# A Strassen level over half of the inner dimension in a gated linear recurrence, with gate functions moved between engines

## The chip, the cores and the metric

One core of a Trainium2 chip runs the whole program. The metric is the device time of one execution in microseconds. The kernel before took 2131.48 us (median of three runs, 2130.56 to 2131.69). Five engines with own instruction queues work in it: TensorE (PE in the profile, its weight loads PEld), VectorE (DVE), ScalarE (ACT), GpSimd (POOL) and SyncE (SP, which here issues DMAs).

## The reference

A decoder trunk of two layers on 1024 tokens of width 1024. The first layer mixes tokens with a gated linear recurrence (HGRN2), the second with sliding-window attention, and each ends with a gated convolutional FFN of width 2816. The change lies in the first mixer:

```python
q, f, i, g = jnp.split(h @ w_in, 4, axis=-1)          # h (1024, 1024), w_in (1024, 4096)
fg = lb + (1.0 - lb) * jax.nn.sigmoid(heads(f))       # 8 heads of 128
o = hgrn2_chunkwise(jax.nn.silu(heads(q)), 1.0 - fg, heads(i), jnp.log(fg))
o = o * lax.rsqrt(jnp.mean(jnp.square(o), -1, keepdims=True) + RMS_EPS)
o = o * g_norm_w * jax.nn.silu(heads(g))
return o.reshape(B, S, D) @ w_out
...
u = h @ w_in                                          # FFN: up, causal conv of width 3, gate, down
return (jax.nn.silu(a) * b) @ w_out
```

The recurrence is `S_t = diag(f_t) S_{t-1} + k_t v_t^T ; o_t = S_t^T q_t` with k = 1 - f and v = i.

## The kernel before

Everything is float32, and a product is made from float32r parts: a tile is split into a high part (ScalarE casts) and a low part (VectorE subtracts, `low_part`, L169), and `mm3` makes three passes hi x hi, hi x lo, lo x hi into one PSUM bank (L194, L195, L196). `T` holds x transposed, [128 of the inner dimension, part, 8 chunks, 1024 tokens], `HL` the split weights in six places, `raw` the three tiles into which weights are loaded. There are four PSUM banks of 512 columns (`psmm`) and two of 1024 (`psax`).

Stages: the start (x is transposed by TensorE in blocks of 128 tokens, `turn_block`, and each block cast and subtracted into T, while the i/g products of head 0 run), then the recurrence over eight heads, the out projection, the FFN of layer 0, attention, and the FFN of layer 1. In the recurrence TensorE makes for head h the projections `qf(h)` (queries and forget gates, transposed, two token halves each, 8 chunks x 3 passes per half), then `ig_block` (values and gates by token blocks, two passes per chunk, L714 and L715; the result is copied by ScalarE, added by VectorE, L677 and L679, and then its PSUM bank is free). Between these run the small matmuls of `recur(h - 1)` (L200): VectorE scales qp and kp from level to level of a binary tree over the 32-token blocks (`update`, L990 to L995), and TensorE makes `scores` of each level, whose results VectorE puts into Ab (L933, L954). At its end come the state sums (L1071, L1073), the output og, and `norm` (L1098 to L1109), for which GpSimd computes two small instructions.

Beside this the kernel prepares the weights of both FFN down projections for a Strassen product: 22 units of four 128 x 512 subtractions each, on VectorE (L1184), loaded into Y and stored to memory (`bsd`). They are spare work: `lay` puts one in where VectorE's planned backlog is short.

The order of all instructions is written out by hand by a planner (`Order`): `od.t` counts TensorE's time from column counts, `od.v` VectorE's backlog, generators are resumed when TensorE's time has come to the times that they yield, and the spare work fills VectorE while `od.v` is under `od.t + 1.5`. What it decides is fixed when the program is built; on the chip each engine runs its rows in this order and waits for semaphores.

## Time and profile before

| quantity | before |
|---|---|
| median of three runs | 2131.48 us |
| profiled execution | 2131.04 us, span 2129.3 us |
| granted TensorE clock | 1.00 |
| TensorE busy | 2119.9 us, 100% of the span |
| VectorE, ScalarE, GpSimd busy | 83%, 44%, 6% |
| stages by the rows | start to 37.6 us, heads to 456, out projection to about 500, then FFN, attention, FFN |
| one head | about 53 us |

A row of the timeline gives start, length, engine, line, operation, what is written from what, shape, and in brackets the idle time ahead of it with what ended it. A row of groups has the count behind x, then the busy time in all, the mean in ns and the idle time ahead. A row of waits has the sum, the count and the longest.

### The profile page before, as it was taken

The numbers are of one execution on the slowest core, as the hardware profiler recorded it, in microseconds if no ns is written. First come the engines' busy times: TensorE is split into PE (matmuls) and PEld (weight loads), VectorE is DVE, ScalarE is ACT, GpSimd is POOL, SyncE is SP. The second block draws the span as 40 slices with busy tenths as digits, with TensorE's granted clock in tenths as the row PEclk, the third lists the DMA queues.
The fourth block names the chain that finished last, engine by engine and source line by source line (L and its number), as shares of the span: only waits on it lengthen the run. The fifth ranks groups of instructions, "written<-read, shape, count | busy, mean of one in ns | idle before, by whom it ended". The sixth has DMA issues, their size and how long they took to land.

```text
span 2129.3 us, 32129 instructions
## 1 busy us (share of the span) xinstructions
PE 2119.9 (100%) x12663; PEld 1779.6 (84%) x12663; DVE 1760.9 (83%) x2375; ACT 926.5 (44%) x1491; POOL 132.5 (6%) x150
## 2 busy tenths in 40 slices
PE   9999999999999999999999999999999999999998
PEld 8888888888888888888888888888888888888887
DVE  4777776677999999887988658969999999978986
ACT  4444444452444444434433356743544444444430
POOL 1000000001100000000001113321000000000002
PEclk9999999999999999999999999999999999999999
DMA  5655443214223222228854411042233222249662
GB/s 216 243 211 169 144 132 119 75 32 177 99 85 98 85 89 79 80 99 275 288 190 161 129 26 45 24 149 89 80 100 98 90 86 83 86 148 325 229 215 90
DMA packets 229838, 278.96 MB, mean 131 GB/s; under 512 B 29960, under 2 KB 158648, under 8 KB 226872
## 3 DMA queue, kind: packets, MB, share of 16 engines
q1 hardware_dynamic: 228736, 276.53, 39.0%
q8 instruction: 99, 1.62, 0.3%
q10 hardware_dynamic: 856, 0.37, 0.1%
q14 instruction: 51, 0.42, 0.1%
q0 software_dynamic: 96, 0.02, 0.0%
HBM read 213.94 MB, written 62.94 MB: 130 GB/s over the span
## 4 chain that ended last, share of the span: by engine, by line
PE 99%; DMA 0%; DVE 0%; SPq 0%; issue 0%; DVEq 0%
PE psmm L194 17%; PE psmm L196 17%; PE psmm L195 17%; PE psax L194 10%; PE psax L196 10%; PE psax L195 10%; PE psmm L714 5%; PE psax L200 4%; PE psmm L715 3%; PE psmm L204 1%; PE psmm L200 1%; PE psax L204 1%; PE psax L1427 1%; PE psmm L1274 1%; DMA Y<-in_x_dram 0%; PE psmm L752 0%
## 5 line engine op out<-in xcount | busy, mean ns | idle before, releaser
L194 PE MATMUL psmm<-T,HL 128*128 128x512 f32 x768 | 303.4, 395 | 0.0
L196 PE MATMUL psmm<-T,HL 128*128 128x512 f32 x768 | 299.4, 390 | 0.0
L195 PE MATMUL psmm<-T,HL 128*128 128x512 f32 x768 | 299.2, 390 | 0.0
L473 DVE SCALAR_TENSOR_TENSOR Y<-Y,cwt 128x1023 f32<-128x1023 f32 (+1 forms) x176 | 225.0, 1281 | 44.3 <-ACT Y L471 42.9
L221 ACT CAST HL<-rx 128x1024 fp32r<-128x1024 f32 (+1 forms) x151 | 150.7, 1007 | 178.3 <-PE psmm L195 30.9
L169 DVE TENSOR_TENSOR HL<-rx,HL 128x1024 fp32r<-128x1024 f32 (+1 forms) x151 | 178.5, 1188 | 16.9 <-ACT HL L221 16.8
L714 PE MATMUL psmm<-HL,T 128*128 128x512 f32 x496 | 176.8, 399 | 0.0
L196 PEld LDWEIGHTS psmm<-T,HL 128*128 128x128 f32 x768 | 144.2, 188 | 30.7
L194 PEld LDWEIGHTS psmm<-T,HL 128*128 128x128 f32 x768 | 144.3, 188 | 29.6 <-issue 0.4
L195 PEld LDWEIGHTS psmm<-T,HL 128*128 128x128 f32 x768 | 144.3, 188 | 28.8 <-issue 0.4
L471 ACT ACTIVATE Y<-Y,cwt 128x1024 f32<-128x1024 f32 x88 | 108.7, 1238 | 101.6 <-DVE Y L460 89.4
L715 PE MATMUL psmm<-HL,T 128*128 128x256 f32 x496 | 138.9, 280 | 0.0
L194 PE MATMUL psax<-T,HL 128*128 128x512 f32 x352 | 137.3, 390 | 0.0
L196 PE MATMUL psax<-T,HL 128*128 128x512 f32 x352 | 137.0, 389 | 0.0
L195 PE MATMUL psax<-T,HL 128*128 128x512 f32 x352 | 137.0, 389 | 0.0
L243 POOL TENSOR_TENSOR rs<-rs,nhalf 128x1 f32<-128x1 f32 x32 | 44.6, 1394 | 1286.6 <-DVE rs L242 1286.6
L714 PEld LDWEIGHTS psmm<-HL,T 128*128 128x128 f32 x496 | 93.1, 188 | 21.0
L715 PEld LDWEIGHTS psmm<-HL,T 128*128 128x128 f32 x496 | 93.7, 189 | 0.4
L221 ACT CAST HT<-rx 128x1024 fp32r<-128x1024 f32 (+1 forms) x37 | 35.5, 960 | 127.9 <-DVE rx L427 76.4
L169 DVE TENSOR_TENSOR HL<-raw,HL 128x1024 fp32r<-128x1024 f32 x51 | 62.1, 1219 | 20.2 <-ACT HL L176 19.3
L195 PEld LDWEIGHTS psax<-T,HL 128*128 128x128 f32 x352 | 66.2, 188 | 13.7
L196 PEld LDWEIGHTS psax<-T,HL 128*128 128x128 f32 x352 | 66.1, 188 | 13.6
(315 smaller groups left out, 5232.3 us busy)
## 6 DMA issues: line engine op xcount, KB each, us to landing
rx<-in_ffn_w_in_dram SPq DMA_DIRECT2D x136, 256.0 KB, 3.2
rx<-gd SPq DMA_DIRECT2D x118, 256.0 KB, 3.9
Y<-in_ffn_w_out_dram SPq DMA_DIRECT2D x44, 512.0 KB, 6.4
bsd<-Y SPq DMA_DIRECT2D x22, 1024.0 KB, 4.8
gd<-Y SPq DMA_DIRECT2D x44, 512.0 KB, 2.6
rx<-in_ffn_w_out_dram SPq DMA_DIRECT2D x54, 256.0 KB, 4.7
R<-bsd SPq DMA_DIRECT2D x44, 256.0 KB, 5.1
Y<-in_ffn_w_in_dram SPq DMA_DIRECT2D x40, 256.0 KB, 2.9
```

Source lines behind the costliest of these rows:

```text
L169: make = lambda e: e.tensor_tensor(lo, src, hi.bitcast(F32), op=ALU.subtract)
L194: nc.tensor.matmul(ps, st(0), mv(0), start=start, stop=False)
L195: nc.tensor.matmul(ps, st(0), mv(1), start=False, stop=False)
L196: nc.tensor.matmul(ps, st(1), mv(0), start=False, stop=stop)
L200: nc.tensor.matmul(ps, lhsT, rhs, start=start, stop=stop, **kw)
L204: nc.tensor.transpose(ps, src, ident)
L221: nc.scalar.copy(hi, src)
L243: nc.gpsimd.tensor_tensor(rs, rs, nhalf, op=ALU.pow)
L471: nc.scalar.activation(c, u, AF.Identity, bias=cwt[:, l, 3, ci:ci + 1], scale=cwt[:, l, 2, ci:ci + 1])
L473: nc.vector.scalar_tensor_tensor(c[:, sh:], u[:, :S - sh], cwt[:, l, 2 - sh, ci:ci + 1], c[:, sh:], op0=ALU.mult, op1=ALU.add)
L714: nc.tensor.matmul(ps, T[:, 0, kc, ts], w[:, :, kc % 4, :], start=kc == 0, stop=False)
L715: nc.tensor.matmul(ps[:, :256], T[:, 1, kc, ts], w[:, 0, kc % 4, :], start=False, stop=kc == KC - 1)
```

## The change

Queries and forget gates of a head are made together. Over chunks 0 to 3 of the inner dimension, the product of x (two token halves by two pairs of chunks) with the weights (two pairs of chunks by q and f) is done by one Strassen level: seven products of two chunks instead of eight. Chunks 4 to 7 stay as they were. The PSUM tiles are pa, ps, pc, pd, and pa again: pa is begun, copied out, added on to, copied out, added on to, read by VectorE, and added on to once more for the late queries. The sums and differences of x are made once at the start, for blocks 4 to 7 while they are transposed: the chunks 0 and 1 of the late tokens hold in T the sum of two chunks, a new tile `Sx` holds three other sums, and GpSimd, VectorE and ScalarE share the work (`x_whole`, `x_sums`). So that i/g blocks can use this T, each head gets a weight difference (`ig_diff`); for the q/f weights there are four small VectorE sums (`qf_sums`), and each head splits one weight tile more of 512 and one of 768 columns.

Silu and Tanh on ScalarE take the place of Sigmoid and a VectorE product. The weight sums for the FFN work in half units in Yx, one row by VectorE as spare work (16 of 44 half units), the other by GpSimd (28), with loads and stores in quarters. Y's place is freed: the first six heads' outputs go to memory (`hod`) and come back into Sx in the last head, the seventh's stays in Yx, and the out projection takes the late token blocks first. The spare work fills up to 2.0 instead of 1.5.

```diff
-        while self.fill and self.v < self.t + 1.5 and self.fill():
+        while self.fill and self.v < self.t + 2.0 and self.fill():
...
+        def ig_diff(raw):
+            d = tail["raw"][2][:, :512]
+            nc.vector.tensor_tensor(d, raw[:, 512:], raw[:, :512], op=ALU.subtract)
+        def qf_sums(q, f):
+            b11, b21, b12, b22 = q[:, :256], q[:, 256:512], f[:, :256], f[:, 256:512]
+            t3, t2, t4 = [tail["raw"][2][:, 256 * i:256 * (i + 1)] for i in range(3)]
+            for x, y, z in ((t3, b22, b12), (b12, b12, b11), (t2, b22, b12), (t4, b21, t2)):
+                nc.vector.tensor_tensor(x, y, z, op=ALU.subtract)
...
                 yield 0.7
-                nc.scalar.activation(sg, G, AF.Sigmoid)
-                yield 0.8
-                nc.vector.tensor_tensor(G, G, sg, op=ALU.mult)
+                nc.scalar.activation(G, G, AF.Silu)
...
+            def x_whole(tb):
+                t0 = slice((tb - 4) * P, (tb - 3) * P)
+                raw = lambda h: T[:, h, :4, t0].bitcast(F32)
+                sub2(fours[tb % 2][0].rearrange("p (k t) -> p k t", k=KC)[:, :4], raw(0), raw(1), op=ALU.add)
+            def x_sums(tb):
...
+                nc.scalar.copy(r[:, 4:6], pv[:, :2])
+                split(T[:, 0, 2:, ts], T[:, 1, 2:, ts], pv[:, 2:])
+                nc.vector.tensor_tensor(r[:, 6:8], r[:, 4:6], pv[:, 2:4], op=ALU.add)
+                sub2(v[:, 1], r[:, :2], r[:, 4:6], op=ALU.subtract)
+                sub2(v[:, 0], r[:, 6:8], r[:, :2], op=ALU.subtract)
+                sub2(v[:, 2], r[:, 2:4], v[:, 0], op=ALU.subtract)
+                split(T[:, 0, :2, ts], T[:, 1, :2, ts], r[:, 6:8])
...
-            for half in range(2):
-                proj_T(weights["f"], half, ps)
-                nc.scalar.activation(fg[:, ts], ps, AF.Sigmoid)
...
+            pa = psmm()
+            add_on(pa, q, 0, tokens(early), 2, start=True)
+            nc.scalar.copy(kp[:, early], pa)
+            ps = psmm()
+            add_on(ps, q, 2, tokens(early, 2), 6, start=True)
+            after(1.0, query_early(ps))
+            add_on(pa, e, 2, sums(0), 2)
+            nc.scalar.copy(fg[:, early], pa)
+            pc = psmm()
+            add_on(pc, f, 0, tokens(late), 2, start=True)
+            nc.scalar.copy(fg[:, late], pc)
+            pd = psmm()
+            add_on(pd, f, 4, tokens(late, 4), 4, start=True)
+            add_on(pa, e, 0, sums(1), 2)
+            after(0.5, third(pa))
+            add_on(pc, f, 4, tokens(early, 4), 4, stop=False)
+            after(0.0, forget_late(pd))
+            add_on(pc, f, 2, sums(2), 2)
+            after(0.5, forget_early(pc))
+            od.finish(mine[1:2])
+            add_on(pa, e, 4, tokens(late, 2), 2, stop=False)
+            add_on(pa, q, 4, tokens(late, 4), 4)
+            nc.scalar.activation(qs[:, late], pa, AF.Silu)
...
+                for us, x, y, z in ((0.69, blocks[:, :2], blocks[:, 1::2], blocks[:, :2]), (0.42, b22, b22, b11), (0.42, b21, b21, b22)):
+                    if r:
+                        sub2(x, y, z, op=ALU.subtract)
+                    else:
+                        pending.append((us, lambda x=x, y=y, z=z: tt(x, y, z, op=sub)))
```

`sub2` is GpSimd's tensor_tensor, `plus` and `third` are VectorE adds of 512 columns (L1010), and `add_on` makes the three passes per chunk (L999).

The order of ScalarE at the start of before, from the cast of block 3 (psax_248) on; psax_292, psax_309 and psax_354 are blocks 4, 5 and 6:

```order
L221 CAST T_81<-psax_248 128x8x128
L696 ACTIVATE VG_169<-psmm_170 128x2x128
L697 COPY VG_169<-psmm_170 128x2x128
L221 CAST T_81<-psax_292 128x8x128
L677 COPY VG_169<-psmm_274 128x256
L221 CAST T_81<-psax_309 128x8x128
L677 COPY VG_169<-psmm_306 128x256
L687 ACTIVATE sg_344<-VG_169 128x256
L221 CAST T_81<-psax_354 128x8x128
```

The same place in the change, where psax_260, psax_308 and psax_334 are blocks 3, 4 and 5, and qs and VG_104 hold copies and sums of chunks:

```order
L221 CAST T_81<-psax_260 128x8x128
L176 CAST HL_82<-raw2_101 128x512
L726 ACTIVATE VG_180<-psmm_181 128x2x128
L727 COPY VG_180<-psmm_181 128x2x128
L836 COPY qs_128<-psax_308 128x256
L221 CAST T_81<-psax_308 128x6x128
L221 CAST T_81<-qs_128 128x2x128
L710 COPY VG_180<-psmm_289 128x256
L836 COPY VG_104<-psax_334 128x256
L221 CAST T_81<-psax_334 128x6x128
L221 CAST T_81<-VG_104 128x2x128
L221 CAST Sx_102<-fg_129 128x3x2x128
```

A block's one cast has become a copy and two casts with a VectorE sum between them; the weight difference's cast stands ahead of block 4, and the cast of the sums that GpSimd makes behind block 5.

The order of TensorE in the change where the second head's projection (psmm_1249 is pa, psmm_1306 pc) runs between two steps of the first head's scores (L200):

```order
L999 MATMUL psmm_1249<-Sx_102,HL_82 128x512 x3
L200 MATMUL psax_1342<-St_1188,one_112 32x256 x4
L200 MATMUL psax_1342<-VG_180,one_112 32x128 x4
L200 MATMUL psax_1342<-kd_1195,one_112 32x256 x4
L200 MATMUL psax_1342<-VG_180 32x16 x32
L200 MATMUL psax_1342<-qp_1184,kp_653 32x16 x32
L999 MATMUL psmm_1249<-Sx_102,HL_82 128x512 x3
L999 MATMUL psmm_1306<-T_81,HL_82 128x512 x12
L999 MATMUL psmm_1306<-Sx_102,HL_82 128x512 x6
L999 MATMUL psmm_1249<-T_81,HL_82 128x512 x3
L200 MATMUL psax_1471<-kd_1422 32x16 x32
```

Where before a projection went on through the passes of one bank, TensorE comes back to pa after 12 and 6 passes elsewhere. The order of VectorE in the change at this place, released by the small matmuls above (psax_1342):

```order
L1143 TENSOR_TENSOR qp_1184<-qp_1184,tot_1185 128x64x8
L1145 TENSOR_TENSOR kp_653<-kp_653,tot_1185 128x64x8
L1148 TENSOR_TENSOR tot_1185<-tot_1185 128x64
L1086 COPY_PREDICATED Ab_116<-msk_79,psax_1342 128x256
L1086 COPY_PREDICATED Ab_116<-msk_79,psax_1342 128x128
L1107 COPY_PREDICATED Ab_116<-msk_79,psax_1342 128x32x4
L1143 TENSOR_TENSOR qp_1184<-qp_1184,tot_1185 128x32x16
L1145 TENSOR_TENSOR kp_653<-kp_653,tot_1185 128x32x16
L1148 TENSOR_TENSOR tot_1185<-tot_1185 128x32
L1107 COPY_PREDICATED Ab_116<-msk_79,psax_1342 128x16x8
L1086 COPY_PREDICATED Ab_116<-msk_79,psax_1342 128x64x2 x2
L1010 TENSOR_TENSOR fg_1247<-fg_1247,psmm_1249 128x512
```

and of before, from its last update of the same kind on:

```order
L990 TENSOR_TENSOR qp_603<-qp_603,tot_604 128x32x16
L992 TENSOR_TENSOR kp_459<-kp_459,tot_604 128x32x16
L995 TENSOR_TENSOR tot_604<-tot_604 128x32
L954 COPY_PREDICATED Ab_113<-msk_79,psax_707 128x16x8
L933 COPY_PREDICATED Ab_113<-msk_79,psax_707 128x64x2 x2
L1184 TENSOR_TENSOR Y_82<-Y_82 128x512
L169 TENSOR_TENSOR HL_83<-raw1_100,HL_83 128x1024
```

Behind the same updates and copies, where a weight sum stood that nobody waits for, there is now the add that reads pa.

GpSimd's order, which in before had in the heads only the norm's pairs:

```order
L169 TENSOR_TENSOR HL<-raw_99,HL 128x1024
L1099 TENSOR_SCALAR ss<-ss 128x8
L1100 TENSOR_TENSOR ss<-ss,nhalf 128x8
L1099 TENSOR_SCALAR ss<-ss 128x8
L1100 TENSOR_TENSOR ss<-ss,nhalf 128x8
```

and in the change, from the second weight half unit that it sums to the norm of the first head:

```order
L1341 TENSOR_TENSOR Yx<-Yx 128x512
L1341 TENSOR_TENSOR Yx<-Yx 128x256 x2
L1341 TENSOR_TENSOR Yx<-Yx 128x512
L1341 TENSOR_TENSOR Yx<-Yx 128x256 x2
L1252 TENSOR_SCALAR ss<-ss 128x8
L1253 TENSOR_TENSOR ss<-ss,nhalf 128x8
L1341 TENSOR_TENSOR Yx<-Yx 128x512
```

The norm's two instructions stand in a queue with weight sums now.

More of the change, by code (lines that the diff above doesn't have):

```diff
@@ L1119, in trunk @@
         lead = [0, 3, 2, 2, 2, 2, 1, 0]
-        begins = [4] + [8 * h + lead[h] for h in range(1, NH)]
-        free, units, loaded, summed = {r: 0 for r in (0, 2, 4, 6)}, list(range(2 * pairs)), [], []
-        slot_no = [-1]
         pending, lowparts, movelows, old = [], [], [], []
@@ L1261, in trunk @@
                 w = nw
-            if units or loaded or pending or summed:
+            od.finish(sums)
+            od.finish(sums)
+            if halves:
                 raise ValueError("a unit is left")
@@ L1307, in ffn @@
                 up = Up(l, pu, tail["raw"])
-                lns = out_proj(us, begun, rows, resid, up, up.ln)
+                lns = out_proj(us, begun, order, rows, resid, up, up.ln)
                 up.run(lns, down)
```

399 lines of the change are left out of this document (262 added, 137 removed).

## The prediction

> **What bounds the kernel now.** I read the page of the whole span first, then the waits of TensorE, then its rows one by one, and last the busy time of the engines by stage.
>
> ```profile
> PE 2119.9 (100%) x12663; PEld 1779.6 (84%) x12663; DVE 1760.9 (83%) x2375; ACT 926.5 (44%) x1491; POOL 132.5 (6%) x150
> PE 99%; DMA 0%; DVE 0%; SPq 0%; issue 0%; DVEq 0%
> PE psmm L809 <- DVE Y L760: 1.0, 1, 1.0
> PE psmm L204 <- DMA Y<-in_x_dram: 0.5, 1, 0.5
> ```
>
> The first line is each engine's busy time, the second the shares of the chain that ended last, and the other two are all that the view of waits has with TensorE as the waiting engine: 1.5 us in the whole execution. TensorE is the path from end to end. So a matmul less is time less, at its spacing and not at its printed length; and whatever makes TensorE wait is time more, one to one, because no other bound stands beside it.
>
> ```profile
> L194 PE MATMUL psmm<-T,HL 128*128 128x512 f32 x257 | 103.3, 402 | 0.0
> 229.27 0.39 PE L194 MATMUL psmm<-T,HL 128*128 128x512 f32 x1
> 229.95 0.39 PE L194 MATMUL psmm<-T,HL 128*128 128x512 f32 x1
> 37.55 0.40 PE L194 MATMUL psmm<-T,HL 128*128 128x512 f32 x1
> 0.00:38.00 38.00, 36.30 (x235) 33.17 (x236) 17.43 (x31) 16.60 (x28) 6.16 (x14) 1.00 0.58 199
> 238.00:288.00 50.00, 50.00 (x398) 43.20 (x397) 37.27 (x68) 21.83 (x51) 1.83 (x2) 1.00 0.41 136
> ```
>
> The first row is the group of first passes of the q/f projections up to 570 us (256 of it belong to the eight heads, the last to the next stage). The next two are two first passes in a row: 0.68 us for a group of three, 0.227 us per pass, though each is printed with 0.39. The fourth is the first such pass of all, at 37.55 us: there the start ends. The last two are busy times in the start and in a piece of a middle head, in the order length, TensorE, its weight loads, VectorE, ScalarE, GpSimd, granted clock: TensorE 50 of 50, VectorE 37 of 50, GpSimd 1.8 of 50. VectorE has a quarter of its time free, but not where it is wanted, as will be seen.
>
> **What the change takes off TensorE.** A head goes from 32 groups of three passes to 30: seven products instead of eight over four of the eight chunks of the inner dimension, two chunks each. The difference of orders agrees: 192 matmuls of T and HL fewer, 144 of Sx and HL more, 48 fewer in eight heads. 48 x 0.227 = 10.9 us. The i/g blocks keep their count. That is the whole gain; all other terms are waits, between 0 and what is worked out below.
>
> **The start.** Blocks 4 to 7 of x no longer go from PSUM to T by one cast and one subtraction.
>
> ```profile
> 18.64 1.00 ACT L221 CAST T<-psax 128x1024 fp32r<-128x1024 f32 x1
> 19.66 1.23 DVE L169 TENSOR_TENSOR T<-psax,T 128x1024 fp32r<-128x1024 f32 x1 [1.61 <-ACT T L221]
> 21.51 0.38 ACT L677 COPY VG<-psmm 128x256 f32<-128x256 f32 x1
> 24.43 0.41 DVE L679 TENSOR_TENSOR VG<-VG,psmm 128x256 f32<-128x256 f32 x1
> 24.51 0.40 PE L714 MATMUL psmm<-HL,T 128*128 128x512 f32 x1
> 43.25 0.60 ACT L900 ACTIVATE fg<-psmm 128x512 f32<-128x512 f32 x1 [2.08 <-PE psmm L196]
> 1397.81 1.28 POOL L1447 TENSOR_TENSOR X<-X,bf 128x512 f32<-128x512 f32 x1 [4.76 <-DVE X L1439]
> 614.29 2.40 POOL L478 TENSOR_TENSOR Y<-Y 128x1024 f32<-128x1024 f32 x1 [5.44 <-DVE Y L473]
> ```
>
> From these rows: ScalarE takes 0.38 us for 256 columns, 0.60 for 512, 1.00 for 1024 (768: about 0.82); VectorE 0.41, 0.68 and 1.23 (768: 0.95); GpSimd 1.28 for 512 and 2.40 for 1024, which makes 0.73 for 256. Block 4 is due at 24.51 (the first of its matmuls before). In the new order ScalarE, after block 3's cast (19.6), waits for VectorE: its low part (20.9) and the weight difference (0.69, so 21.6). Then it casts the difference (22.2), does the two first-value functions (23.0), copies two chunks (23.3) and casts six (24.1); VectorE takes their low part (25.1) and adds the sum (25.5); ScalarE casts that (25.8), and its low part ends at 26.2. TensorE reads those two chunks first: it waits 1.6 us where it waited none. Block 5 comes out just in time. Block 6 hangs on GpSimd: its sums for block 5 can't end before 30.4 (five instructions of 0.73 and one of 1.28, the first of them behind the 25.5 above); ScalarE's cast of them stands ahead of block 6's copy and casts, which with VectorE's three parts take another 4.5 us: 34.9. TensorE, after two blocks of 2.84 us and 1.6 us of transposes from 26.1, is there at 33.4: 1.5 us. Block 7 in the same way is 0.45 late, and the first groups of the first head wait about 0.6 for the third weight tile, whose cast and low part stand behind block 7's. Sum 4.15 us, where the profile of before has a quarter of VectorE and a half of ScalarE idle: it is a chain of turns between two engines, not their load. Lower end 1.6 (block 4 alone; the rest gone if GpSimd starts earlier than I place it), upper end 7 (every hand-over 0.1 us longer, the GpSimd sums held up by VectorE).
>
> **The heads.** The tile pa is summed into four times and stays open through the whole projection. Its third value is read by a VectorE add (L1010) before TensorE may go on in it. In the order of before, nothing of TensorE waited for a VectorE read in this place, since each half took a new bank out of four.
>
> ```profile
> 236.42 0.50 PE L194 MATMUL psmm<-T,HL 128*128 128x512 f32 x1
> 236.54 0.69 DVE L990 TENSOR_TENSOR qp<-qp,tot 128x512 f32<-128x512 f32 x1 [3.81 <-PE psax L200]
> 239.66 0.69 DVE L992 TENSOR_TENSOR kp<-kp,tot 128x512 f32<-128x512 f32 x1
> 240.68 0.93 DVE L933 COPY_PREDICATED Ab<-msk,psax 128x128 f32<-128x128 uint8 x2
> 242.11 0.70 PE L200 MATMUL psax<-kd 128*32 128x16 f32 x62
> 243.38 0.69 DVE L990 TENSOR_TENSOR qp<-qp,tot 128x512 f32<-128x512 f32 x1 [0.53 <-PE psax L200]
> 246.16 0.68 DVE L910 TENSOR_TENSOR qs<-qs,psmm 128x512 f32<-128x512 f32 x1
> 254.05 0.29 DVE L1071 COPY St<-psax 128x128 f32<-128x128 f32 x1 [6.08 <-PE psax L200]
> 267.47 1.22 DVE L1102 TENSOR_TENSOR og<-og,ss 128x1024 f32<-128x1024 f32 x1
> 271.43 1.22 DVE L1001 TENSOR_TENSOR St<-qs,kp 128x1024 f32<-128x1024 f32 x1
> 277.56 0.41 DVE L679 TENSOR_TENSOR VG<-VG,psmm 128x256 f32<-128x256 f32 x1
> ```
>
> TensorE leaves the fourth step's small matmuls at 236.4; VectorE, released then, works through two updates and the copies till 241.6. In the second head's order the L1010 add stands right behind these copies, so it ends at 242.2, and TensorE comes back to pa 21 passes later, 236.4 + 4.8 = 241.2: a wait of 0.9 us with its hand-over. In the third and fifth projections 24 passes, small matmuls and 9 or more passes lie between, and there is room. In the fourth and sixth the add stands behind updates 5 and 6 (end 246.2, so 246.8) and pa is due at 246.4: 0.4 each. 1.6 us together. The scores themselves (242.1, fed by the row that ends at 240.35) keep their 1.8 us. The adds that free the i/g blocks' banks stand behind the opening of a head, which before ran from 271.43 to 277.56 with no wait of TensorE, and in two heads now behind the norm's product (1.22) too: 0 to 1.2 us there, I take the middle, 0.6. Sum 2.2 us.
>
> What costs nothing:
>
> ```profile
> L1184 DVE TENSOR_TENSOR Y<-Y 128x512 f32<-128x512 f32 x88 | 60.1, 690 | 1.5
> L689 DVE TENSOR_TENSOR VG<-VG,sg 128x256 f32<-128x256 f32 x31 | 13.2, 425 | 9.1 <-ACT sg L687 9.0
> L910 DVE TENSOR_TENSOR qs<-qs,psmm 128x512 f32<-128x512 f32 x16 | 11.0, 686 | 12.9 <-ACT qs L907 12.9
> 17.23 1.28 ACT L830 ACT_TABLE_LOAD   x1
> ```
>
> These three VectorE groups, 84 us, go. In their place come 16 half units of sums (24 us by the durations above), 32 adds of 0.68 (22), 32 small sums of 0.41 (13), 8 differences of 0.68 (5) and 16 low parts (13): 77 us, so VectorE's load in a head stays near 37 of 50. ScalarE gains three copies of 0.60 a head and is at 22 of 50. The table loads are five before and four after, none inside a head, and the one that goes lay beside matmuls. The weight halves' loads and stores are 88 and 88 quarters against 44 and 22; no step of TensorE waits for them. Head outputs take a way through memory and are back a whole head before the out projection. The stages behind 500 us have the same instructions.
>
> **The price that before barely shows: GpSimd beside VectorE.** Contrary to its label, the change gives VectorE 16 of the 44 half units of weight sums and GpSimd 28, each of one 512 and two 256 columns: 1.28 + 2 x 0.73 = 2.75 us, 77 us in the heads where GpSimd was near idle.
>
> ```profile
> 1398.22 1.42 DVE L169 TENSOR_TENSOR T<-Y,T 128x512 fp32r<-128x512 f32 x1
> 1409.20 0.68 DVE L169 TENSOR_TENSOR T<-Y,T 128x512 fp32r<-128x512 f32 x1
> 614.64 3.13 DVE L169 TENSOR_TENSOR HL<-rx,HL 128x1024 fp32r<-128x1024 f32 x1
> L169 DVE TENSOR_TENSOR HL<-raw,HL 128x1024 fp32r<-128x1024 f32 x51 | 62.1, 1219 | 20.2 <-ACT HL L176 19.3
> ```
>
> A VectorE subtraction of 0.68 us took 1.42 where GpSimd's add of 1397.81 ran, and ended 0.55 us after it; one of 1.22 took 3.13 beside the GpSimd row of 614.29. So VectorE loses up to what is left of a GpSimd instruction. Bounds in a head: nothing, if the 3.5 batches fall into VectorE's idle stretches (3.81 and 6.08 us above), up to 2.75 each where they fall into the 4 us before pa or the scores. I take nothing on top of the 2.2, by the nearest row: the idle stretches are longer than a batch. The Trainium skill, page "SBUF — State Buffer", section "SBUF: two separate sides", calls the port pair of these two engines "an exclusive lock, not a bandwidth split", held by whichever starts first, against a VectorE instruction with two SBUF inputs. The rows above agree: 1.42 and 3.13 are waits to the end, not slower work. By that rule the sums on GpSimd would be no relief of VectorE but 77 us taken from it, and the change would end as in the third rival below.
>
> **Sum.** 2131.04 (the profiled execution, span 2129.3 and 1.7 around it; the median of the runs is 0.44 higher) - 10.9 + 4.15 + 2.2 = 2126.5 us. A change under 0.2%, 4.3 us, is about what this kernel's measurement can't tell from none.
>
> **Rivals.**
> 1. Nearly all is kept. Waits that I work out from hand-overs overlap: a late block 4 gives every later chain its 1.6 us back, and a pa add that runs in an idle stretch of VectorE costs nothing. Then the start costs 1.6 and the heads none: 2131.04 - 10.9 + 1.6 = 2121.7. For it speaks that TensorE waited for nothing in the heads before, with VectorE at 37 of 50; against it, that the start's chain has no idle to give.
> 2. It evens out. Start 6, heads 5 (0.7 a head: pa late in every head, not in three): 2131. For it: pa's margins above are 0 or below in three of six heads.
> 3. Slower, by the hold of GpSimd on VectorE. If in each of seven heads one batch falls between 236.5 and 241.6, the two updates and pa's add come 2.75 us later less what is free, 1.8 us at the scores and nothing at pa: 1.7 us a head, 12 us; with the start at 7 it is 2131.04 - 10.9 + 12 + 7 = 2139. With the start at 4.15, the gain is used up from 6.7 us in the heads, 0.96 a head, and the kernel is measurably slower from 1.6 a head. Against it: GpSimd's batches wait for loads, and are not tied to that place.
> 4. It does less than it says: a group of Sx passes could be spaced wider than 0.227. With the same tiles' shape and type I give that 0.02, inside rival 2.
>
> **Chances.** Forecast 0.40 (own range 2123.5 to 2130), rival 1 0.18 (2119.5 to 2123.5), rival 2 0.18 (2130 to 2135.3), rival 3 0.24 (above 2135.3). The forecast lies across the bound of 0.2% (2127.2): 0.27 of it below. Faster 0.18 + 0.27 = 0.45, same 0.13 + 0.18 = 0.31, slower 0.24. The range from 2120.5 to 2138.5 leaves out about 0.05 below and 0.12 above.
>
> **What would show it.** The q/f passes of L999 must number 720, 48 fewer than the 768 of before, and stand 0.227 apart. The first of them should come at 37.55 + 3.5 or more, with TensorE waiting for T in the blocks before; earlier than 39.5 and the start is rival 1's. In the heads, waits of TensorE for L1010 would show pa, for L712 the banks, for L1143 or L1145 the scores; VectorE rows of 0.68 printed with 1.4 to 2.0 beside L1341 rows would show rival 3. The prediction is wrong if TensorE's waits in the heads are above 7 us, or below 0.5 with a start that lost nothing.

## The result and the profile after

The changed kernel takes 2183.53 us (median of four runs, 2180.35 to 2187.3) against 2131.28 us for the kernel before on the same chip: ratio 1.0244, 95% interval 1.0231 to 1.0257. It is 52 us slower, where 4.5 us faster was forecast (2126.5 against the profiled 2131.04). The profiled execution took 2186.52 us, its span is 2184.5 us. The four executions differ by up to 7 us and the profiled one is among the longer, so pieces of a few us in the comparisons below carry some of this spread.

From the page of the kernel after: busy time by engine, shares of the chain that ended last, and the group of GpSimd's new sums.

```profile
PE 2129.2 (97%) x12615; PEld 1780.3 (81%) x12615; DVE 1797.5 (82%) x2392; ACT 950.2 (43%) x1546; POOL 250.7 (11%) x250
...
PE 86%; DVE 8%; ACT 3%; issue 1%; DMA 1%; POOL 0%; SPq 0%; ACTq 0%; DVEq 0%; POOLq 0%
...
L1341 POOL TENSOR_TENSOR Yx<-Yx 128x256 f32<-128x256 f32 (+1 forms) x84 | 100.2, 1193 | 253.3 <-DMA Yx<-in_ffn_w_out_dram 248.9
```

TensorE has its 48 passes less (12663 to 12615) and yet more busy time, mostly because a part of them ran at a slower clock, as shown below; it carried 99% of the chain before and carries 86% now. VectorE has 8% of the chain at an unchanged share of busy time. GpSimd's 28 half units took 100.2 us, 3.58 each, not 2.75.

The waits of TensorE after (sum, count, longest); before, the whole view had 1.5 us, and now it has 47.4:

```profile
PE psmm L744 <- DVE VG L712: 9.9, 5, 2.8
PE psmm L204 <- DVE Y L255: 7.9, 1, 7.9
PE psax L200 <- ACT kd L1211: 7.9, 4, 3.8
PE psmm L999 <- DVE fg L1010: 6.4, 4, 2.5
PE psax L200 <- issue: 3.6, 2, 2.8
PE psmm L999 <- DVE VG L712: 2.9, 2, 2.5
PE psmm L744 <- ACT T L221: 2.3, 2, 1.5
```

Three kinds stand out: VectorE is late for the banks (L712) and for pa (L1010); ScalarE is late with kd (L1211); and at the out projection the first LayerNorm is late (L255). For the 3.6 us put down to issue the profile names no cause.

Where in the program the time went shows in one row per kernel of the view of line 200, here the first and last start of the small score matmuls (before, then after); the table has the same for four of the experiments told below:

```profile
L200 PE MATMUL psax<-qp,kp x768: 182/186/201, 76.7 to 456.6; 128*32 128x16 f32 x128, 128*32 128x32 f32 x64
```

```profile
L200 PE MATMUL psax<-qp,kp x768: 176/186/241, 81.0 to 498.6; 128*32 128x16 f32 x128, 128*32 128x32 f32 x64
```

| kernel | first | last | between them | behind the last, to the end of the span |
|---|---|---|---|---|
| before | 76.7 | 456.6 | 379.9 | 1672.7 |
| after | 81.0 | 498.6 | 417.6 | 1685.9 |
| e1, GpSimd's sums left out | 80.1 | 466.5 | 386.4 | 1683.6 |
| e2, kd copied by VectorE | 82.9 | 487.0 | 404.1 | 1683.3 |
| e4, before with sums on GpSimd | 82.6 | 477.6 | 395.0 | 1672.6 |
| e6, e1 and e2 and e5 | 78.4 | 458.3 | 379.9 | 1683.3 |

So of the 55.2 us between the two spans, 4.3 lie ahead of the first scores, 37.7 in the heads, 13.2 behind them. Between the first and the last scores stand 39 of the 48 passes saved, 8.9 us at 0.227, so the heads lost more than the 37.7 show.

How the waits come about is read from the timeline. Three places of TensorE after, in three different heads:

```profile
144.55 0.96 PE L999 MATMUL psmm<-T,HL 128*128 128x512 f32 x3 [2.54 <-DVE fg L1010]
...
159.88 1.38 PE L200 MATMUL psax<-VG,kd 128*128 128x128 f32 x10 [2.25 <-ACT kd L1211]
...
183.50 0.79 PE L744 MATMUL psmm<-HL,T 128*128 128x512 f32 x1 [2.78 <-DVE VG L712]
```

The third has VectorE and GpSimd ahead of it, at the opening of a head:

```profile
175.54 4.62 POOL L1341 TENSOR_TENSOR Yx<-Yx 128x512 f32<-128x512 f32 x3 [0.35 <-DMA Yx<-in_ffn_w_out_dram]
...
176.10 2.31 DVE L1155 TENSOR_TENSOR qp<-qs,fg 128x1024 f32<-128x1024 f32 x1
178.45 1.11 DVE L1159 TENSOR_TENSOR VG<-kp,qp 128x512 f32<-128x512 f32 x1
179.59 1.12 DVE L1143 TENSOR_TENSOR qp<-qp,fg 128x512 f32<-128x512 f32 x1
...
183.04 0.41 DVE L712 TENSOR_TENSOR VG<-VG,psmm 128x256 f32<-128x256 f32 x1
```

One batch of GpSimd takes 4.62 us, and the three VectorE rows that overlap it 4.54 where such rows take 1.22 + 0.68 + 0.68 alone: both engines lose. VectorE's add for the bank comes 2 us later for it, and TensorE waits 2.78. Over all heads the two rows of the view of groups that are the same in both kernels (before, then after) say it in one number, 686 ns against 832:

```profile
L992 DVE TENSOR_TENSOR kp<-kp,tot 128x512 f32<-128x512 f32 x48 | 32.9, 686 | 0.0
```

```profile
L1145 DVE TENSOR_TENSOR kp<-kp,tot 128x512 f32<-128x512 f32 x48 | 39.9, 832 | 0.0
```

The second place of TensorE above waits for ScalarE, whose queue stands so:

```profile
153.47 0.63 ACT L1014 ACTIVATE fg<-fg 128x512 f32<-128x512 f32 x1
...
157.10 0.72 ACT L1017 ACTIVATE kp<-fg,one 128x512 f32<-128x512 f32 x1
157.85 0.60 ACT L1068 ACTIVATE qs<-psmm 128x512 f32<-128x512 f32 x1
158.35 0.57 ACT L1124 COPY A<-psax 64x512 f32<-64x512 f32 x1
158.81 1.01 ACT L1211 COPY kd<-psax 128x1024 f32<-128x1024 f32 x1
```

Between the first two rows stand four more of the same kind (L1014, L1015 and L1017 for each half): six gate functions, one Silu and a copy without a gap ahead of the copy of kd, which ScalarE made before too, but not at the end of such a row.

Last, the clock. Busy times in stretches of 5 us of the kernel after (TensorE, its weight loads, VectorE, ScalarE, GpSimd, granted clock, DMA share, GB/s), behind waits of 2.54, 2.25, 3.77 and 7.93 us, in this order; only behind the second is the clock full. The last stretch has the end of its wait in it:

```profile
145.00:150.00 5.00, 5.00 (x108) 4.09 (x107) 3.86 (x4) 0.62 (x1) 2.71 (x3) 0.66 0.21 70
...
160.00:165.00 5.00, 5.00 (x35) 4.58 (x36) 3.04 (x9) 0.47 (x2) 0.81 (x1) 1.00 0.67 228
...
345.00:350.00 5.00, 5.00 (x21) 4.71 (x22) 1.64 (x5) 0.27 (x1) 0.00 (x0) 0.50 0.70 234
...
575.00:580.00 5.00, 2.66 (x11) 2.47 (x12) 4.46 (x6) 1.22 (x3) 0.90 (x1) 0.50 0.75 266
```

A long wait can cost twice: first itself, then some microseconds at a lower clock. Each 5 us times what its clock lacks to 1.00, added up over 145 to 590 us, is 17.1 us. About 2.6 of these lie inside the wait of 7.93 itself (570 to 577.3 us) and are left out, which leaves 14.5. With 45.9 us of waits more than before and the 10.9 us of passes saved this makes 49.5 of the 55.2 us of the spans. The rest is not shown. An estimate for most of it: a pass is printed with 0.39 us but spaced 0.227, and a wait is counted from the printed end, so each of the 26 waits more takes about 0.16 us besides, 4 us in all.

### The profile page after: what moved, and what is told of

It reads as the page before. It is cut to its first block, busy times and chain, and to the rows that moved or that the text cites. A ratio compares the mean times of both kernels' runs of the same rounds, so it can differ in the third digit from the quotient of the medians.

```text
span 2184.5 us, 32426 instructions
## 1 busy us (share of the span) xinstructions
PE 2129.2 (97%) x12615; PEld 1780.3 (81%) x12615; DVE 1797.5 (82%) x2392; ACT 950.2 (43%) x1546; POOL 250.7 (11%) x250
## 4 chain that ended last, share of the span: by engine, by line
PE 86%; DVE 8%; ACT 3%; issue 1%; DMA 1%; POOL 0%; SPq 0%; ACTq 0%; DVEq 0%; POOLq 0%
PE psmm L194 14%; PE psmm L196 14%; PE psmm L195 14%; PE psax L194 9%; PE psax L196 9%; PE psax L195 9%; PE psmm L999 5%; PE psax L200 3%; PE psmm L744 2%; PE psmm L204 2%; PE psmm L200 1%; PE psax L1630 1%; DVE qp L1143 1%; PE psmm L1475 1%; DVE kp L1145 1%
## 5 line engine op out<-in xcount | busy, mean ns | idle before, releaser
L194 PE MATMUL psmm<-T,HL 128*128 128x512 f32 x512 | 200.5, 392 | 0.0
L196 PE MATMUL psmm<-T,HL 128*128 128x512 f32 x512 | 199.3, 389 | 0.0
L195 PE MATMUL psmm<-T,HL 128*128 128x512 f32 x512 | 199.3, 389 | 0.0
L744 PE MATMUL psmm<-HL,T 128*128 128x512 f32 x496 | 183.0, 409 | 12.5 <-DVE VG L712 9.9
L999 PE MATMUL psmm<-T,HL 128*128 128x512 f32 x576 | 144.9, 400 | 10.7 <-DVE fg L1010 6.4
L999 PEld LDWEIGHTS psmm<-T,HL 128*128 128x128 f32 x576 | 107.5, 191 | 35.7 <-DVE fg L1010 8.1
L1341 POOL TENSOR_TENSOR Yx<-Yx 128x256 f32<-128x256 f32 (+1 forms) x84 | 100.2, 1193 | 253.3 <-DMA Yx<-in_ffn_w_out_dram 248.9
L196 PEld LDWEIGHTS psmm<-T,HL 128*128 128x128 f32 x512 | 96.1, 188 | 19.9
L195 PEld LDWEIGHTS psmm<-T,HL 128*128 128x128 f32 x512 | 96.2, 188 | 19.7
L194 PEld LDWEIGHTS psmm<-T,HL 128*128 128x128 f32 x512 | 96.1, 188 | 19.6
```

The costliest lines, as they stand in the source:

```text
L194: nc.tensor.matmul(ps, st(0), mv(0), start=start, stop=False)
L195: nc.tensor.matmul(ps, st(0), mv(1), start=False, stop=False)
L196: nc.tensor.matmul(ps, st(1), mv(0), start=False, stop=stop)
L744: nc.tensor.matmul(ps, T[:, 0, kc, ts], w[:, :, k, :], start=kc == 0, stop=False)
L999: nc.tensor.matmul(ps, w[:, wi, w0 + k, :], mv(mi, k), start=start and k + j == 0, stop=stop and k == n - 1 and j == 2, skip_group_check=True)
L1341: sub2(x, y, z, op=ALU.subtract)
```

## Experiments

Theory A: the loss is owed to GpSimd's sums, which hold VectorE back (the third rival of the prediction, at a much larger size). Theory B: it is owed to the new order of the heads and the new hand-overs (pa, the gate functions), and the sums on GpSimd matter little. Beside both stand two single causes: the copy of kd behind ScalarE's burst, and the out projection.

**e1: GpSimd's sums left out.** The loads and stores stay; the sums of 28 of the 44 half units are not made. VectorE, ScalarE and SyncE have the same instructions in the same order as in the change.

```diff
                     if r:
-                        sub2(x, y, z, op=ALU.subtract)
+                        pass
```

> The changed kernel without the 28 half units of weight sums on GpSimd (left out: those sums; their loads and stores stay, and no other engine's order changes). Theory A (GpSimd's instructions hold VectorE up, and that is most of what the heads lose): the 100 us of GpSimd's L1341 go, VectorE's L1143/L1145 come back from 0.78/0.83 to 0.69 us, TensorE's waits between 80 and 500 us fall from about 33 us to under 12, and the time falls by 25 us or more, to under 2159. Theory B (the turns of the new order, one engine behind another, make the waits, and GpSimd only lengthens them): waits of 20 us and more stay, and the time stays above 2165.

2150.38 us, ratio 1.0084 (1.0067 to 1.0100): 33 us less than the change whole. The waits of e1:

```profile
PE psmm L204 <- DVE Y L255: 6.6, 1, 6.6
PE psax L200 <- ACT kd L1211: 3.8, 4, 1.9
PE psax L200 <- issue: 3.2, 1, 3.2
PE psmm L744 <- ACT T L221: 2.2, 2, 1.4
PE psmm L744 <- DVE VG L712: 1.7, 2, 0.8
```

All waits together are 22.0 us, and the sum for the clock is 8.5. L712 is down from 12.8 to 2.5 us in its two rows (the second, not shown, has 0.8), L1010 from 6.4 to 0.7, kd from 7.9 to 3.8, and the group of VectorE that took 832 ns is back:

```profile
L1145 DVE TENSOR_TENSOR kp<-kp,tot 128x512 f32<-128x512 f32 x48 | 33.0, 687 | 0.0
```

In the table above, 31.2 of its gain lie between the first and the last scores. That is theory A, for 33 of the 57 us between forecast and result.

**e2: the copy of kd on VectorE.**

```diff
-            nc.scalar.copy(kd, ps)
+            nc.vector.tensor_copy(kd, ps)
+            od.vec(1.2)
```

> The changed kernel with the copy of kd out of PSUM (L1211) on VectorE instead of ScalarE, where it stands behind six gate functions and a Silu that come in one burst. If that queue is the cause, TensorE's four waits for L1211 (7.9 us) go, and with them the stretches at half clock behind the two long ones: 8 to 13 us less, about 2172. If VectorE is as late as ScalarE there, the waits are named for VectorE and the time is within 4 us of 2183.5.

2175.12 us, ratio 1.0208 (1.0192 to 1.0223), 8.4 us less. The wait for kd falls from 7.9 to 0.2 us, that for L712 (both rows) grows from 12.8 to 16.6, and that for L1010 falls from 6.4 to 3.2: VectorE is late for the banks instead, and it is still a gain. The planner, which is told of VectorE's 1.2 us, also gives a few weight sums, loads and stores other places, so the edit is not the copy alone.

**e3: at the first out projection the low parts of the late out weights (TX) earlier on VectorE.**

```diff
+                forced = dh == 0 and n < 4 and order is not None and order[0] == 4
+                with tc.manual_schedule(engines={EN.DVE}) if forced else nullcontext():
+                    if forced:
+                        for u in ((0, 1), (), (2,), (3,))[n]:
+                            out_late(late, rows, u, ff.TX)
```

> The changed kernel with VectorE's low parts of the out projection's second half of weights (TX) put ahead of most of the residual adds, as they stood before the change. If their place behind seven adds is what delays the next loads, the row loads and so the first LayerNorm, the one TensorE wait of 7.9 us at 577 us and the slow clock behind it go: 8 to 12 us less, about 2173. If instead the late loads of x do it, nothing changes (within 3 us).

2184.23 us, ratio 1.0248 (1.0233 to 1.0264). The low parts came at 547 us instead of 549, so the edit did not do what it was for, and the wait of 7.1 us stayed: it tells nothing.

**e4: the kernel before, with 14 of the 22 units of its weight sums on GpSimd,** each at the same place of the order.

```diff
+                eng = nc.gpsimd.tensor_tensor if i % 11 < 7 else tt
...
-                    pending.append(lambda x=x, y=y, z=z: tt(x, y, z, op=sub))
+                    pending.append(lambda x=x, y=y, z=z, eng=eng: eng(x, y, z, op=sub))
```

> The kernel before with 14 of its 22 units of weight sums on GpSimd instead of VectorE (56 instructions of 512 columns, some 72 us, the same place in the order; nothing else changes). VectorE gets 39 us less to do. Theory A: two-input instructions of VectorE wait for GpSimd to end, VectorE's updates lengthen, TensorE begins to wait in the heads, and the time grows by 5 to 25 us. Theory B: with the old order's reserves of about 2 us the hold is absorbed: TensorE's waits stay under 3 us and the time is within 3 us of 2131.3.

2153.94 us, ratio 1.0104 (1.0089 to 1.0119): 22.8 us slower than before, in the old order, with the old hand-overs. From its page, its groups between 38 and 520 us, and its waits:

```profile
PE 2125.6 (99%) x12663; PEld 1783.4 (83%) x12663; DVE 1769.0 (82%) x2319; ACT 926.8 (43%) x1491; POOL 223.5 (10%) x206
```

```profile
L1185 POOL TENSOR_TENSOR Y<-Y 128x512 f32<-128x512 f32 x56 | 91.0, 1631 | 49.5 <-DMA Y<-in_ffn_w_out_dram 46.4
```

```profile
PE psmm L714 <- DVE VG L679: 7.0, 2, 4.5
PE psax L200 <- DVE kp L992: 3.4, 1, 3.4
```

56 subtractions of 690 ns, 38.6 us, were taken off VectorE, and its busy time rose from 1760.9 to 1769.0 us: the other instructions grew by 46.7 us beside 91.0 us of GpSimd. All of the loss lies ahead of the last scores (behind them 1672.6 us, as before). VectorE's updates are longer in the heads here too, 775 ns against 686:

```profile
L992 DVE TENSOR_TENSOR kp<-kp,tot 128x512 f32<-128x512 f32 x48 | 37.2, 775 | 0.0
```

GpSimd's norm, which now stands behind weight sums in its queue, is not the cause: VectorE waits for its result once, 3.3 us, as before. So sums on GpSimd alone, by holding VectorE up, make a kernel slower that has nothing else of the change.

**e5: the TX low parts on GpSimd** instead of VectorE, for the same wait as e3.

```diff
-                    out_late(late, rows, n, ff.TX)
+                    out_late(late, rows, n, ff.TX, nc.gpsimd if order[0] else None)
```

> The changed kernel with the low parts of the out projection's second half of weights (TX) on GpSimd, which is idle there, so that they no longer stand in VectorE's queue behind adds that wait for TensorE (in e3 they still did, at 547 us instead of 549). If their place holds up the next loads through the shared tiles, the fourth weight load starts about 8 us earlier, the row load with it, TensorE's wait of 7.9 us before its first transposes of the FFN goes with the half clock behind it: 8 to 12 us less than 2183.5. If the loads of x or another tile hold it up, the wait stays above 5 us and the time within 3 us.

2183.39 us, ratio 1.0243; the low parts now start at 533.7 us instead of 549.0, and the wait stays at 7.0 us. So their place in VectorE's queue is not what it hangs on. SyncE's queue holds the load of `HL<-gd`, which waits for the out products, ahead of the loads of the first feed-forward weights (548.2 and 548.6 us), and the bias row of the LayerNorm comes behind those at 566.6, where before it had come at 512.9.

**e6: e1, e2 and e5 together.** Their three edits.

> The changed kernel with three causes taken away at once: no weight sums on GpSimd (28 half units left out, as in e1), kd on VectorE (e2), TX's low parts on GpSimd (e5). If the waits add up as the traces say, TensorE waits for about 8 us in all, the Strassen level gives its 10.9, the start costs its 4: 2150.4 less 6 (kd and its clock) less 9 (out projection) makes about 2135, with 2130 as what would show the gain net. If the causes overlap (one wait hides another), it stays above 2142.

2144.05 us, ratio 1.0063 (1.0047 to 1.008), 9 us above what was expected and in the range foreseen for causes that overlap.

```profile
PE psmm L204 <- DVE Y L255: 8.2, 1, 8.2
PE psmm L744 <- ACT T L221: 2.3, 2, 1.4
PE psax L200 <- issue: 2.2, 1, 2.2
PE psmm L744 <- DVE VG L712: 1.9, 2, 1.1
```

By the table, the heads now take exactly what they took before, 379.9 us, and 10.6 of the remaining 12.3 us of the spans lie behind them, at the out projection. That is still without a gain from the 39 passes fewer that stand in the heads: 6.9 us of waits are left between the first and the last scores.

**e7: e6 with all 44 half units on VectorE,** so that nothing is left out.

```diff
-                    if r:
-                        sub2(x, y, z, op=ALU.subtract)
+                    if False:
+                        pass
...
-                yield 1.0 if r else 2.5
+                yield 2.5
```

> As e6, but whole: all 44 half units of weight sums on VectorE as spare work, none on GpSimd. VectorE gets 43 us more in the heads. Theory A (GpSimd's hold was the loss, not VectorE's load): within 6 us of e6, so about 2138. Theory B (VectorE has no room: its queue is what makes TensorE wait): 15 us or more above e6, 2150 and over.

2267.59 us, ratio 1.0639 (1.0623 to 1.0655), and a miss of its own kind: 16 half units, more than were thought, had found no place by the end of the recurrence and were made there one by one while TensorE stood.

```profile
588.50 2.93 PE L1479 MATMUL psmm<-HL,T 128*128 128x512 f32 x6 [113.26 <-DVE VG L712]
```

Ahead of this stop its heads had 27 half units on VectorE instead of the 16 of e6, and took 386.9 us between first and last scores instead of 379.9: 11 half units more were not free there. e11 was made to have all of them within the heads.

**e8: the kernel before with Silu and Tanh alone.**

```diff
-                nc.scalar.activation(sg, G, AF.Sigmoid)
-                yield 0.8
-                nc.vector.tensor_tensor(G, G, sg, op=ALU.mult)
-                od.vec(0.4)
+                nc.scalar.activation(G, G, AF.Silu)
...
-                nc.scalar.activation(fg[:, ts], ps, AF.Sigmoid)
+                nc.scalar.activation(fg[:, ts], ps, AF.Tanh, scale=0.5)
```

> The kernel before with only the gate functions changed (Silu and Tanh on ScalarE in place of Sigmoid and a VectorE product, 47 VectorE instructions and 24 us fewer). Both theories: TensorE did not wait in the heads before, so nothing to gain; within 3 us of 2131.2. A loss above that would say that the gates' place in ScalarE's queue costs by itself.

2131.69 us, ratio 1.0003 (0.9993 to 1.0012). The gate functions cost and bring nothing by themselves; VectorE's products were under cover.

**e9, e10, e11: the out projection's queues put in the order of the code.** In e9 the change whole, with SyncE at the first out projection in the order of the code, the raw tiles begun anew, and the TX low parts on GpSimd; e10 is e9 with e1's and e2's edits (so without GpSimd's sums, as e12 to e14 are); e11 is e10 with the sums made, 37 half units on VectorE with shorter pauses and spare work up to 2.5, and 7 on GpSimd in the last head.

```diff
+        if order[0]:
+            ring["raw"] = 0
...
-        for dh in range(2):
+        with tc.manual_schedule(engines={EN.SP}) if order[0] else nullcontext():
+            for dh in range(2):
```

> The changed kernel with three edits at the out projection only: the rotation of the weight tiles starts at the first one again (as before the change, where the recurrence ended on another tile), SyncE's loads there go in the order of the program (the FFN weights ahead of the row of HL that waits for the out products), and TX's low parts on GpSimd. e5 did the last alone, and the row of the LayerNorm's bias still came 14 us later against the out products than before the change, behind the load that waits for HL. If that queue is the cause, the wait of 7 to 8 us before the first transposes of the FFN goes with its half clock: 8 to 13 us less, about 2172. If not, within 3 us of 2183.5.

> e9 with kd on VectorE (e2) and without the 28 half units of weight sums on GpSimd (left out, as in e1). e6 (2144.1) with the out projection mended: 8 us of wait and some 4 us of half clock less, about 2131 to 2134. That would make the Strassen level's 10.9 us just pay for the start (4), the 7 us of waits that stay in the heads and the clock behind them.

> e10 made whole: the weight sums on VectorE with shorter pauses between the steps of a unit and spare work up to 2.5 us, and only the last seven half units or so on GpSimd, in the last head. e7 (2267.6) had left 11 half units to the end of the recurrence, in one burst of 113 us on VectorE that TensorE waited out, while its heads up to 450 us had few waits. Theory A (GpSimd's hold, not VectorE's load): within 8 us of e10, 2131 to 2142. Theory B (VectorE has no room for 37 half units): above 2150.

e9: 2188.11 us, ratio 1.0264 (1.0249 to 1.028). e10: 2150.36, ratio 1.0089 (1.0074 to 1.0104), 6 us worse than e6. e11: 2172.24, ratio 1.019 (1.0173 to 1.0207). The wait on L255 was 5.8, 6.2 and 5.8 us, and a new one of about 3 us came up on a weight tile: no repair. e11 less e10 is 22 us for sums that VectorE must make nearly alone:

```profile
PE psmm L747 <- DVE VG L715: 9.2, 4, 4.3
```

(L715 is the line that was L712.) So theory B has a part too: in the new heads VectorE cannot make them at no cost either, though by its busy time a quarter of a head was free. What the seven half units on GpSimd cost of the 22 us is not separated.

**e12, e13, e14: VectorE's order at the out projection by hand as well,** on the base of e10, the low parts on VectorE again. e12 takes the order of the code; e13 has the four low parts first and the first feed-forward weights' sums behind the eight adds; e14 puts these sums ahead of the eighth add and issues the second weights' loads around the bias row.

```diff
-        with tc.manual_schedule(engines={EN.SP}) if order[0] else nullcontext():
+        with tc.manual_schedule(engines={EN.SP, EN.DVE}) if order[0] else nullcontext():
```

> The kernel of e10_all_three (kd copied by VectorE, the 28 half units that GpSimd would sum left out, SyncE's queue at the out projection in the order of the code), with two things changed: the low parts of the late out weights (TX) go back to VectorE, and VectorE too follows the order of the code at the out projections (each low part stands ahead of the add of its block, and the casts and sums of the first feed-forward weights ahead of the last four adds). e10 measured 2150.4 with PE waits of 6.2 us on Y L255 and 2.9 us on HL L169 there, e6_three_undone 2144.05 with 8.2 us on Y L255. Theory A: the first LayerNorm is late because the loads of the first feed-forward weights (line 419 here) start at 509 us instead of 494 us, for they want the raw tiles that the late low parts hold; with the low parts in time these loads start at 496 to 500 us, the bias row's at 515 to 520 us, the wait on L255 is below 2 us, the slow clock behind it is gone, and the kernel takes 2130 to 2138 us. Rival: the wait comes from elsewhere (VectorE's order itself, the LayerNorm's place in TensorE's order, the later end of the heads): the wait on L255 stays above 4 us and the time is 2142 us or more.

> As e12_out_order, but VectorE's order at the first out projection is the one the kernel before had: the four late low parts first, then all eight adds of the first half of the columns (one cast of the feed-forward weights between them), then the sums of the first feed-forward weights, the bias row, and the second weights only after two LayerNorms. In e12_out_order the row came 5 us earlier than in e10_all_three, and the wait on Y L255 still grew to 15.8 us, because the casts and sums stood ahead of the last adds and waited for ScalarE. Theory A: what TensorE waits for at the out projection is VectorE's order there and the loads it holds back, nothing else; then the wait on L255 is below 2 us, the slow clock behind it is gone, and with the 10.9 us of passes, the start and the head adds the kernel takes 2130 to 2137 us. Rival: the wait is owed to the later heads or to ScalarE's casts: above 4 us on L255, and 2142 us or more.

> As e13_out_as_before, with two corrections: SyncE issues the loads of the second feed-forward weights around the bias row, as the kernel before does, and no longer behind the stores of the first LayerNorms; and the sums of the first feed-forward weights stand ahead of the eighth add instead of behind it. In e13 the wait on Y L255 had fallen to 4.5 us (three waits, none above 1.8), but the late weights made new ones (7.7 us on line 397 and 4.9 us on line 340, behind casts whose loads were issued at 541 us instead of 514). Theory A (the order of VectorE and SyncE at the out projection is what is left): the new waits go, all waits of the stage 480 to 620 us come to 4 us at most, and the time is 2132 to 2140 us. Rival: waits of 8 us or more stay in that stage under this order too, and the time is above 2144 us; then what is left is not owed to the order of these two queues alone.

2165.61 us (ratio 1.016, 1.0143 to 1.0177), 2168.75 (1.0169, 1.0152 to 1.0186) and 2160.98 (1.0142, 1.0125 to 1.0159): all three worse than e10. One row for each says how the wait wandered.

```profile
PE psmm L204 <- DVE Y L255: 15.8, 4, 11.6
```

```profile
PE psmm L194 <- DVE Y L397: 7.7, 1, 7.7
```

```profile
PE psmm L194 <- DVE Y L345: 5.9, 3, 4.8
```

The order of VectorE's queue does move the waits from line to line, with single ones of up to 11.6 us; but none of these orders is the one the kernel before has, e13's neither, though it was meant to be: before, sums, low parts, adds and statistics are mixed more finely. What the stage would cost in that order stays open.

## Why the prediction was wrong

**The passes: right.** L999 has 576 and 144 passes, 720 as stated, 48 fewer, and their median spacing is 0.227 us as before. Where TensorE does not wait they are worth what was put down.

**The start: right in size, a little too dear.** Forecast were 3.55 us for the blocks and 0.6 for the third weight tile. Two waits for blocks 4 and 6, and the first passes after:

```profile
24.65 0.50 PE L744 MATMUL psmm<-HL,T 128*128 128x512 f32 x1 [0.80 <-ACT T L221]
...
34.14 0.51 PE L744 MATMUL psmm<-HL,T 128*128 128x512 f32 x1 [1.48 <-ACT T L221]
...
40.47 1.55 PE L999 MATMUL psmm<-T,HL 128*128 128x512 f32 x6
...
42.41 1.88 PE L999 MATMUL psmm<-T,HL 128*128 128x512 f32 x7 [0.39 <-DVE VG L712]
```

40.47 instead of 37.55 is 2.9, and 0.4 more behind it: 3.3 for 4.15. The chain of turns between ScalarE and VectorE was the right reading, and the 1.5 us of block 6 came as worked out (1.48). Block 4 cost 0.80 and 0.15 more instead of 1.6, block 7 nothing instead of 0.45, and the 0.39 in the first groups are owed to a bank (L712), not to the third weight tile.

**GpSimd beside VectorE: the step that failed.** The text had the price in its own rows (0.68 against 1.42, 1.22 against 3.13) and then put down nothing, "the idle stretches are longer than a batch". That VectorE has room somewhere in a head does not make a batch fall there. A batch starts when its loads land, on no clock of VectorE's, and the instructions that it meets belong to chains on which TensorE hangs. e4 measured 22.8 us for 91.0 us of GpSimd work in the old order, e1 33 us for 100.2 us in the new. The third rival had the mechanism and missed the size: 1.7 us a head with one batch in each, 12 us in all, where 31.2 of the 37.7 us by which the heads grew went with the sums. It looked at one place of a head; the waits came at several (banks, pa, kd). The section of the Trainium skill that the prediction cites ("SBUF — State Buffer", "SBUF: two separate sides") spoke for that rival, and e4 agrees with what follows from it: VectorE got busier when work was moved off it. That both sides lose (a batch 3.58 instead of 2.75) agrees too. But GpSimd is not all of this step: with nearly all sums on VectorE they still cost 22 us in the new order (e11 over e10). The spare time that the text counted on was not free for either engine.

**The heads' own hand-overs: 1.6 + 0.6 forecast, right in kind, near in size by luck.** With the sums left out (e1) L1010 costs 0.7 and L712 2.5, 3.2 us against 2.2. But the split is another, and the places are others. The text had pa late in the second, fourth and sixth projections and saw room in the third and fifth; TensorE waited for it in the first, third, fifth and seventh, the third being the row of 144.55 shown above:

```profile
58.42 9.82 PE L999 MATMUL psmm<-T,HL 128*128 128x512 f32 x42 [0.76 <-DVE fg L1010]
...
273.36 0.97 PE L999 MATMUL psmm<-T,HL 128*128 128x512 f32 x3 [1.02 <-DVE fg L1010]
...
399.72 0.96 PE L999 MATMUL psmm<-T,HL 128*128 128x512 f32 x3 [2.10 <-DVE fg L1010]
```

In e1 only the one in the third is left (0.67). In the change whole the two lines have 6.4 and 12.8. The prediction called itself wrong if TensorE waited more than 7 us in the heads, and it waited 36.

**ScalarE: costed at nothing, wrong.** "ScalarE gains three copies of 0.60 a head and is at 22 of 50" is a share of busy time. The burst of gate functions ahead of kd was in the order and was not looked for. It cost 7.9 us of waits; e2 got 8.4 us back. About half of these waits (4.1 us) went with GpSimd's sums in e1 too, so the two causes overlap. e8 shows that in the old order the functions themselves cost nothing; it is their place in the queue that does.

**The out projection: costed at nothing, wrong.** "The stages behind 500 us have the same instructions" is true of what is computed, not of the order. The change takes the late token blocks first there, and the order of VectorE and SyncE is another: the late weights' low parts, two of which stood ahead of the first add before, stand behind seven adds, and the bias row of the first LayerNorm came late. This is 7.9 us of waiting, and 13.2 us behind the last scores in all. Which single difference is to blame is not shown: six edits (e3, e5, e9, e12, e13, e14) left the waits or moved them, and the new order of the blocks was not tested by itself.

**The clock behind a wait: not foreseen.** Some 14.5 us by the stretches of 5 us, inside the figures above. It is the reason why e1's 33 us are more than the 25 us by which the waits fell (47.4 to 22.0): the sum for the clock fell by 8.6 us beside them.

The sum as it came out, in spans: 55.2 = 4.3 ahead of the first scores, 37.7 in the heads (31.2 of them gone with GpSimd's sums in e1, the other 6.5 in e6, mostly with kd), 13.2 behind. None of the variants of the change beat the kernel before; the best that computes everything is e11 at 2172.24, the best at all e6 at 2144.05 with the sums left out.

## What to carry to other kernels

Work given to GpSimd was not taken off VectorE here (e4: 38.6 us off, 46.7 us back): price such an instruction as work on VectorE at a moment that VectorE cannot choose, and ask which chain it meets there, not whether the engine has idle time. Read the order of each queue ahead of every copy on which TensorE hangs, ScalarE's too, and do it for the stages behind the change as well when a scheduler lays them out. On a kernel that is all TensorE, a wait of more than 2.5 us mostly cost itself and part of the next microseconds.

## What the runs showed of the hardware

- In the changed kernel, of the waits of TensorE from 2.5 us up (2.52, 2.54, 2.78, 2.83, 2.78, 3.77 and 7.93 us) all but the first were followed by 5 us stretches at a granted clock of 0.50 to 0.86; none of the waits from 1.0 to 2.25 us was. The Trainium skill, page "TensorE: Matmul & The Clock Gate", section "HAM oscillation — how this bites in real kernels", warns of gaps above about 3.4 us; here shorter ones were followed by it too. The length of one wait does not settle it: the changed kernel had 0.66 from 500 to 505 us behind waits of 0.90 and 0.37 only, and e1 had 0.66 from 35 to 40 us behind one of 1.44, where the changed kernel kept 1.00 behind one of 1.48.
- VectorE and GpSimd both get slower side by side: GpSimd's 512-column sum took 1631 ns on average in e4 against 1.28 us in the single row of before (1397.81), and VectorE's 512-column update 832 ns in the change and 775 in e4 against 686.
